# Casting the second layer's weights DRAM to DRAM during the first layer, and splitting the first layer's write-back over two blocks

## The chip, the cores and the metric

The kernel runs on all eight cores of one Trainium2 chip. Every core computes one sequence of the batch with its own copy of the weights' bf16 form, and no core waits for another. The metric is the device time of the slowest core in microseconds (us). A program of eight cores has a faster and a slower state: in some executions the cores of one die, or of both, get a lower TensorE clock, and the time is some per cent longer.

Engines: TensorE (PE: matmuls), VectorE (DVE), ScalarE (ACT), GpSimd (POOL) and SyncE (SP, which here only issues DMAs). A DMA issued by SyncE or ScalarE goes to one queue each; a DMA that changes the type, f32 to bf16, is issued by GpSimd and goes to a queue of its own (q0 in the profile; SyncE's is q1).

## The reference, cut to what matters

Two layers over 2048 tokens of width 2048, f32 inputs and weights:

```
shift, scale, gate = Linear(silu(c))              # adaLN
h   = x * (1 + scale) + shift
P   = h @ W_in                                    # 11.8k mixer columns, 8k merge-gate columns
y_A = Mamba-2 SSD; y_B = sliding-window attention
y_C = gated short convolution; y_D = RG-LRU
m   = sum_k sigmoid(G_k(h)) * (y_k @ W_branch[k])
x   = LayerNorm(alpha * x + gate * (m @ W_out))
```

Per layer there are 214 MB of f32 weights, 107 MB as bf16. MB and GB here are 10^6 and 10^9 bytes, as in the profile; only the sizes of single tiles and of single DMAs (KB, and the MB of `w`, `wg` and `wo` below) are counted in 1024s.

## The kernel before

Each layer works through four blocks of 512 tokens. The first half of a block makes `h` and the four branches and needs 92 weight tiles `w` (1 MB f32, 0.5 MB bf16). The second half merges and projects and needs 64 tiles `wg` (1.5 MB f32) and 16 tiles `wo` (1 MB f32). All operations are recorded in program order; then a list scheduler that runs when the kernel is built decides each engine's fixed order, by a key and by its own reckoning of durations. The second half of block s is keyed to run beside the first half of block s+1. I call this a pair: pair 0 is the second half of block 0 with the first half of block 1, and so on to pair 6. Blocks 0 to 3 are layer 0, blocks 4 to 7 are layer 1; so pair 3 holds the first half of layer 1's first block, pair 4 its second half.

The weights come as f32 and are multiplied as bf16. At a layer's first block each tile is cast on its way in, and written back as bf16 to scratch DRAM for the three blocks that follow:

```python
    def load_w(pool, l, first, src, scr, rscr, nel):      # first: t == 0
        w, rw = pool.get()
        wf = w.rearrange("p a b -> p (a b)")[:, 0:nel]
        if first:
            P.dma("pool", wf, src, writes=[rw], nbytes=128 * nel * 4)              # f32 -> bf16, on-chip
            P.dma("sp", scr, wf, reads=[rw], writes=[rscr], nbytes=128 * nel * 2)  # write-back
        else:
            P.dma("sp", wf, scr, reads=[rscr], writes=[rw], nbytes=128 * nel * 2)
        return w, rw
    ...
    NW1, NWG = 4, 3                                       # buffers for w, and for wg and wo
    ...
    for l in range(DEPTH):
        for t in range(NT):
            stage1(l, t)                                  # first half
            if prev is not None:
                stage2(*prev)                             # second half of the block before
            prev = (l, t)
```

adaLN for layer 0 (twelve blocks of w_ada, eight for scale and shift, four for the gate) runs at the start. That of layer 1 is spread over pairs 1 and 2.

The softmax here doesn't subtract the row's maximum and nothing guards it: scores larger than these inputs give would overflow.

Of the kernel before, what the change touches and what calls it, by code (L numbers as in the profile page):

```python
# [71 lines left out]
class Op:  # L72
    __slots__ = ("eng", "fn", "cost", "key", "idx", "preds", "order", "dma", "tbl", "succ", "osucc", "npred",
                 "ready", "sem", "val", "clk", "t0")


class Prog:


    LAT = {"pe": 0.20, "act": 0.22, "dve": 0.20, "pool": 0.25}  # L80
# [3 lines left out]
    DMA_RATE = 280e3  # L84
# [7 lines left out]
    def _add(self, e, fn, reads, writes, cost, acc, dma, tbl):  # L92
        o = Op()
        o.eng, o.fn, o.cost, o.key, o.idx, o.dma, o.tbl = e, fn, cost, self.key, len(self.ops), dma, tbl
        sync, order = set(), set()
        ops = self.ops
        isdma = dma is not None

        def need(i, war):
            p = ops[i]  # L100
            if war and p.dma is None and p.eng == e and not isdma and e == "pe":
                order.add(i)
            else:
                sync.add(i)
        for r in reads:
            for i in r.w:
                need(i, False)
            if r.excl:
                for i in r.r:
                    if ops[i].eng != e:  # L110
                        sync.add(i)
        for r in writes:
            if acc:
                for i in r.pw:
                    need(i, True)
                for i in r.pr:
                    need(i, True)
                for i in r.r:
                    need(i, True)
                if r.w and ops[r.w[-1]].eng == e and not isdma:  # L120
                    order.add(r.w[-1])
            else:
                for i in r.w:
                    need(i, e == "pe")
                for i in r.r:
                    need(i, True)
        k = o.idx
        for r in reads:
            r.r.append(k)
        for r in writes:  # L130
            if acc:
                r.w.append(k)
            else:
                r.pw, r.pr = r.w, r.r
                r.w, r.r = [k], []
        sync.discard(k)
        order.discard(k)
        o.preds, o.order = sync, order - sync
        ops.append(o)
        return o  # L140
# [4 lines left out]
    def dma(self, q, out, in_, reads=(), writes=(), nbytes=0, acc=False):  # L145
        return self._add(q, (out, in_), reads, writes, self.DMA_ISSUE[q], acc, nbytes, None)
# [93 lines left out]
    def emit(self, order):  # L240
        nc = self.nc
        sem = {k: nc.alloc_semaphore("s_" + k) for k in self.eng}
        cnt = {k: 0 for k in self.eng}
        seen = {k: {} for k in self.eng}
        dsem = {q: [[nc.alloc_semaphore("d_%s_%d" % (q, i)), 0, None] for i in range(n)]
                for q, n in self.DMA_SEMS.items()}
        dptr = {q: 0 for q in dsem}
        sems = {}
        last = {}
        ops = self.ops  # L250
        self.nwait = 0
        for o in order:
            e = o.eng
            eng = self.eng[e]
            sn = seen[e]
            slot = None
            ps = [ops[i] for i in o.preds]
            if o.dma is not None:
                slot = dsem[e][dptr[e] % len(dsem[e])]
                dptr[e] += 1  # L260
                if slot[2] is not None:
                    ps.append(slot[2])
            ps.sort(key=lambda p: -p.t0)
            for p in ps:
                if sn.get(p.sem, 0) < p.val:
                    eng.wait_ge(sems[p.sem], p.val)
                    self.nwait += 1
                    for kk, vv in p.clk.items():
                        if sn.get(kk, 0) < vv:
                            sn[kk] = vv  # L270
                    if sn.get(p.sem, 0) < p.val:
                        sn[p.sem] = p.val
            if o.dma is not None:
                slot[1] += 16
                s = slot[0]
                o.sem, o.val = s.name, slot[1]
                sems[s.name] = s
                eng.dma_start(out=o.fn[0], in_=o.fn[1]).then_inc(s, 16)  # L278
                slot[2] = o
            else:  # L280
                ins = o.fn(eng)
                cnt[e] += 1
                s = sem[e]
                sems[s.name] = s
                ins.then_inc(s, 1)
                o.sem, o.val = s.name, cnt[e]
            o.clk = dict(sn)
            last[o.sem] = o.val
        sp = self.eng["sp"]
        for nm, v in last.items():  # L290
            if seen["sp"].get(nm, 0) < v:
                sp.wait_ge(sems[nm], v)
# [15 lines left out]
def build_program():  # L308
# [5 lines left out]
    w_ada = dt_in("w_ada", [DEPTH, 12, NKC, 128, 512])  # L314
# [38 lines left out]
    PM = Pool("pm", [banks[b] for b in (0, 1, 2)])  # L353
    PJ = Pool("pj", [banks[b] for b in (3, 4)])
    PX = Pool("px", [banks[b] for b in (5, 6, 7)])
# [21 lines left out]
    NW1, NWG = 4, 3  # L377
# [61 lines left out]
    def c_dve(n):  # L439
        return 0.16 + n * 1.04e-3  # L440

    def c_act(n):
        return 0.18 + n * 0.85e-3
# [16 lines left out]
    def stt(out, in0, scalar, in1, op0, op1, reads, writes, n=512, acc=False):  # L460
        P.op("dve", lambda e: e.scalar_tensor_tensor(out=out, in0=in0, scalar=scalar, in1=in1, op0=op0, op1=op1),  # L461
             reads, writes, cost=c_dve(n) + 0.03, acc=acc)
# [25 lines left out]
    MMC = 0.2165  # L488

    def load_w(pool, l, first, src, scr, rscr, nel):  # L490
        w, rw = pool.get()
        wf = w.rearrange("p a b -> p (a b)")[:, 0:nel]
        if first:
            P.dma("pool", wf, src, writes=[rw], nbytes=128 * nel * 4)
            P.dma("sp", scr, wf, reads=[rw], writes=[rscr], nbytes=128 * nel * 2)
# [3 lines left out]

    def proj(l, t, hb, idx):  # L500
        w, rw = load_w(WS1, l, t == 0, w1_in[l, idx], w1s[l, idx], rW1S[l][idx], NKC * 128)
# [62 lines left out]
    def ada_piece(l, blk, kc, acc_t, slot, q):  # L564
        (a, ra), (w, rw) = acc_t, slot
        P.dma(q, w, w_ada[l, blk, kc], writes=[rw], nbytes=262144)
# [89 lines left out]
    def mix_a(l, t, setk):  # L656
# [35 lines left out]
        for g in range(4):  # L692
# [4 lines left out]
            for wi, (dst, rdst, col, ci) in enumerate(((bt, rbt, A_B, 8 + g), (ct, rct, A_C, 12 + g))):  # L697
                setk(6 * g + wi)
# [7 lines left out]
                if wi == 0:  # L706
# [6 lines left out]
                    PX.put((px, rpx))  # L713
            xs, zs, ya = [], [], []
            for i in range(2):
                j = 2 * g + i
                setk(6 * g + 2 + 2 * i)
# [8 lines left out]
                setk(6 * g + 3 + 2 * i)  # L726
# [4 lines left out]
                zs.append((z, rz))  # L731
            ya = [PX.get(), PX.get()]
            for u in range(4):
# [67 lines left out]
                HB.put((xe, rxe))  # L801
            BB.put((bc, rbc), (bt, rbt), (ct, rct))
# [22 lines left out]
    def mix_b(l, t, setk):  # L825
# [27 lines left out]
        for kc in range(2):  # L853
            setk(kc)
# [3 lines left out]
            for i in range(2):  # L858
                kh = 2 * kc + i
                P.dma("act", KD[64 - 64 * i:128 - 64 * i, kh, 128:640], KD[64 * i:64 * i + 64, kh, 128:640],  # L860
                      reads=[rKD[kh]], writes=[rKD[kh]], nbytes=65536)
        for v in range(2):
            setk(2 + v)
            idx = TIDX[B_V + 128 * v]
            w, rw = load_w(WS1, l, first, w1_in[l, idx], w1s[l, idx], rW1S[l][idx], NKC * 128)
# [7 lines left out]
            PJ.put((pj, rpj))  # L873
        for jq in range(8):
            kh = jq // 2
            setk(4 + 2 * jq)
# [4 lines left out]
            setk(5 + 2 * jq)  # L881
# [41 lines left out]
            F.put((f, rf))  # L923
        F.put((co, rco), (si, rsi))

    def mix_c(l, t, setk):
# [3 lines left out]
        for j in range(8):  # L930
            setk(4 * j)
# [4 lines left out]
            setk(4 * j + 1)  # L936
# [6 lines left out]
            setk(4 * j + 2)  # L943
# [6 lines left out]
            setk(4 * j + 3)  # L950
# [3 lines left out]
            F.put((a, ra))  # L954

    def mix_d(l, t, setk):
# [3 lines left out]
        for jp in range(4):  # L960
            st = []
            for j in (2 * jp, 2 * jp + 1):
                setk(2 * j)
# [27 lines left out]
            for j, (a, ra), (cv, rcv), (xs, rxs) in st:  # L991
                setk(2 * j + 1)
# [10 lines left out]
                F.put((a, ra), (cv, rcv), (xs, rxs))  # L1003


    def merge_dc(l, t, dc):
# [3 lines left out]
        for k in range(4):  # L1010
            idx = dc * 4 + k
            w, rw = load_w(WSG, l, t == 0, wg_in[l, idx], wgs[l, idx], rWGS[l][idx], 24 * 128)
# [25 lines left out]
    def out_dc(l, t, dc, sums):  # L1038
        s = l * NT + t
        b = s % 2  # L1040
        w, rw = load_w(WSG, l, t == 0, wo_in[l, dc], wos[l, dc], rWOS[l][dc], NKC * 128)
# [54 lines left out]
    def stage1(l, t):  # L1096
        s = l * NT + t
        P.key = s - 0.12
        make_h(l, t)
        base = [0]  # L1100

        def setk(i):
            P.key = s + (base[0] + i) / NTL
        setk(0)
        if t == 0:
            layer_consts(l)
        mix_a(l, t, setk)
        base[0] = 24
        mix_b(l, t, setk)
        base[0] = 44  # L1110
        mix_c(l, t, setk)
        base[0] = 76
        mix_d(l, t, setk)
# [22 lines left out]

    def stage2(l, t):
        s = l * NT + t
        tot = 64 * 24 + 256.0
        for dc in range(NKC):  # L1140
            P.key = s + 1 + 96 * dc / tot
            if l == 0 and t in (1, 2):
                ada_bg(6)
            merge_dc(l, t, dc)
        sums = (F2.get(), F2.get())
        for dc in range(NKC):
            P.key = s + 1 + (1536 + 16 * dc) / tot
            out_dc(l, t, dc, sums)
        P.key = s + 2
# [4 lines left out]
    ring = Pool("adaw", [take([512], F32, at=o_y[0] + i * 2048) for i in range(16)])  # L1154
    accs = Pool("adaa", [take([512], F32, at=o_y[1] + i * 2048) for i in range(12)])
    for _, r in ring.free_:
        pass
    alias0, alias1 = [], []
    for blk in range(12):
        P.key = -1.9 if blk < 8 else 0.4  # L1160
        acc_t = accs.get()
        for kc in range(NKC):
            slot = ring.get()
            alias0.append(slot[1])
            ada_piece(0, blk, kc, acc_t, slot, "sp" if kc % 2 == 0 else "act")
            ring.put(slot)
# [4 lines left out]
        if blk == 11:  # L1171
            ada_post(0, "gate")
# [21 lines left out]
    order = P.schedule()  # L1194
# [80 lines left out]
def make_in_maps(inp, cores):  # L1275
# [4 lines left out]
    wa = np.stack([wa[:, :, c:c + 512].reshape(DEPTH, NKC, 128, 512) for c in blocks], axis=1)  # L1280
# [35 lines left out]
```

## Time and profile before

The first three of the four runs gave 7065.18, 7064.13 and 7385.76 us; the last of these is a slow one. The lines below are from the profile's page: the span, TensorE's busy time with its share of the span and its instructions, and the DRAM traffic.

```profile
span 7077.5 us, 93078 instructions; the slowest of 8 cores (7022.1 to 7077.5 us)
PE 6284.8 (89%) x31128; PEld 2851.3 (40%) x31128; DVE 3735.2 (53%) x5916; ACT 2047.0 (29%) x3257; POOL 540.4 (8%) x1086
...
HBM read 1285.35 MB, written 249.82 MB: 217 GB/s over the span
```

TensorE is 89% busy. To see where the other 11% is, the next view cuts the span into stretches. I matched the recorded operations to the trace by their count on each engine's semaphore, and cut where the last matmul of each block's layer norm ends. Columns: from and to, length, busy time of each engine (with instructions), granted clock of TensorE, share of the DMA engines' time that is busy, GB/s that they moved (bytes written). The rows are start-up, block 0 alone, pairs 0 to 6, and the last second half.

```profile
core 7: us, PE busy (x) PEld busy (x) DVE busy (x) ACT busy (x) POOL busy (x), PEclk, DMA share, GB/s
0.00:265.00 265.00, 23.86 (x101) 22.10 (x102) 164.70 (x266) 13.49 (x22) 6.39 (x14) 1.00 0.92 249
265.00:894.00 629.00, 453.19 (x2151) 192.23 (x2148) 284.87 (x472) 181.12 (x296) 83.35 (x183) 0.87 0.84 176
894.00:1735.00 841.00, 762.54 (x3765) 342.42 (x3765) 414.70 (x647) 247.66 (x399) 79.87 (x168) 0.96 0.88 208
1735.00:2546.00 811.00, 782.34 (x3943) 358.01 (x3942) 494.61 (x786) 251.42 (x403) 59.39 (x93) 0.98 0.62 191
2546.00:3362.00 816.00, 778.54 (x3926) 355.97 (x3925) 489.86 (x777) 253.28 (x404) 56.85 (x93) 0.99 0.63 191
3362.00:4171.00 809.00, 769.55 (x3813) 349.46 (x3812) 427.28 (x685) 250.91 (x398) 81.34 (x184) 0.98 0.90 215
4171.00:5076.00 905.00, 815.75 (x4087) 368.19 (x4086) 451.14 (x734) 283.03 (x451) 87.25 (x180) 0.96 0.90 217
5076.00:5844.00 768.00, 740.61 (x3695) 337.23 (x3693) 409.45 (x631) 231.86 (x371) 35.16 (x83) 0.99 0.51 159
5844.00:6634.00 790.00, 768.88 (x3881) 350.69 (x3880) 427.76 (x674) 251.85 (x403) 50.77 (x88) 0.99 0.52 159
6634.00:7078.00 444.00, 389.48 (x1780) 175.03 (x1777) 170.84 (x247) 82.38 (x116) 0.00 (x0) 0.94 0.46 156
```

A pair without casts (5 and 6, mean 779 us) is 97% TensorE. Start-up, block 0 alone, pair 0 and pair 4 are longer.

The page's lines for DMAs (what, queue, count, KB each, median us from issue to landing) show what a weight buffer goes through at a layer's first block: the cast load, then the write-back.

```profile
arena<-wg POOLq DMA_DIRECT2D x128, 768.0 KB, 11.4
wg_scr<-arena SPq DMA_DIRECT2D x128, 768.0 KB, 10.3
arena<-w POOLq DMA_DIRECT2D x184, 512.0 KB, 9.3
w_scr<-arena SPq DMA_DIRECT2D x184, 512.0 KB, 8.5
```

### The profile page before, as it was taken

What the parts mean: (1) busy time and instruction counts of PE and PEld (TensorE: products, weight loads), DVE (VectorE), ACT (ScalarE), POOL (GpSimd) and SP (SyncE); (2) the same over time, 40 slices, a digit from 0 to 9 for tenths busy, and PEclk for the clock granted to TensorE, in tenths of its full rate; (3) what the DMA queues carried; (4) which work ended last, traced back from release to release, by engine and by line L of the source; (5) the groups of instructions that cost most, each with busy time, mean ns of one, the idle gap of its engine ahead of it and who ended that gap; (6) DMA issues with size and microseconds to landing.
All of it is one profiled execution on the core that took longest, in us unless ns stands there. A gap on an engine that the chain in (4) does not pass through costs nothing.

```text
span 7077.5 us, 93078 instructions; the slowest of 8 cores (7022.1 to 7077.5 us)
## 1 busy us (share of the span) xinstructions
PE 6284.8 (89%) x31128; PEld 2851.3 (40%) x31128; DVE 3735.2 (53%) x5916; ACT 2047.0 (29%) x3257; POOL 540.4 (8%) x1086
## 2 busy tenths in 40 slices
PE   0467788998999989999899988999799999999898
PEld 0232334343444434444344434444344444444343
DVE  5654345526775467635655365543575247643524
ACT  0231233214421243213432243213342134312312
POOL 0010111001100011000110001000010001000000
PEclk9988999999999999999999999999899999999999
DMA  9796989799665566556988999888854456544445
GB/s 260 187 184 153 205 190 212 198 215 242 196 188 190 177 208 194 174 191 183 212 214 205 221 229 207 214 214 206 226 165 142 152 170 188 155 142 161 147 152 162
DMA packets 409845, 1350.35 MB, mean 191 GB/s; under 512 B 49312, under 2 KB 60704, under 8 KB 409376
## 3 DMA queue, kind: packets, MB, share of 16 engines
q1 hardware_dynamic: 308736, 1048.25, 46.0%
q0 software_dynamic: 49824, 214.06, 19.9%
q10 hardware_dynamic: 50816, 82.09, 5.5%
q8 instruction: 257, 4.21, 0.2%
q14 instruction: 212, 1.74, 0.1%
HBM read 1285.35 MB, written 249.82 MB: 217 GB/s over the span
## 4 chain that ended last, share of the span: by engine, by line
PE 72%; DMA 12%; DVE 7%; issue 4%; ACT 3%; ACTq 1%; POOL 1%; SPq 0%; DVEq 0%; POOLq 0%
PE ps L481 72%; DMA arena<-cum_scr 4%; DVE arena L461 3%; DVE arena L457 2%; ACT arena L453 2%; DMA arena<-w 1%; DMA arena<-w_ada 1%; ACTq L278 1%; DVE arena L472 1%; DMA wg_scr<-arena 1%; DMA arena<-arena 1%; DMA arena<-pos 1%; DMA arena<-w_scr 1%; DMA arena<-x 1%; DMA arena<-x_scr 1%
## 5 line engine op out<-in xcount | busy, mean ns | idle before, releaser
L481 PE MATMUL ps<-arena 128*128 128x512 bf16 (+4 forms) x30744 | 6262.4, 366 | 740.5 <-DVE arena L461 307.0
L481 PEld LDWEIGHTS ps<-arena 128*128 128x128 bf16 (+2 forms) x30744 | 2816.3, 102 | 4138.8 <-issue 1279.3
L457 DVE TENSOR_TENSOR arena<-arena 128x512 f32<-128x512 f32 (+4 forms) x2466 | 1473.6, 624 | 635.6 <-ACT arena L453 418.3
L453 ACT ACTIVATE arena<-arena 128x512 f32<-128x512 f32 (+3 forms) x1495 | 946.0, 669 | 1495.0 <-DVE arena L461 384.2
L461 DVE SCALAR_TENSOR_TENSOR arena<-arena,ps 128x512 f32<-128x512 f32 (+1 forms) x832 | 565.2, 687 | 1354.0 <-PE ps L481 1035.1
L461 DVE SCALAR_TENSOR_TENSOR arena<-arena 128x512 f32<-128x512 f32 (+3 forms) x1283 | 934.2, 738 | 502.7 <-ACT arena L453 377.3
L453 ACT ACTIVATE arena<-ps 128x512 f32<-128x512 f32 (+3 forms) x960 | 538.5, 567 | 1660.4 <-PE ps L481 1413.8
L453 ACT ACTIVATE arena<-ps,arena 128x512 f32<-128x512 f32 x648 | 444.9, 687 | 1717.5 <-PE ps L481 1683.0
L457 DVE TENSOR_TENSOR arena<-ps,arena 128x256 bf16<-128x256 f32 (+5 forms) x616 | 262.2, 457 | 440.2 <-PE ps L481 434.9
L475 POOL COPY arena<-arena 128x3 f32<-128x3 f32 (+3 forms) x542 | 210.6, 392 | 3664.4 <-DVE arena L457 1676.2
L472 DVE RECIPROCAL arena<-arena 128x512 f32<-128x512 f32 x80 | 268.0, 3350 | 40.1 <-ACT arena L453 35.6
L461 DVE SCALAR_TENSOR_TENSOR arena<-ps,arena 128x512 f32<-128x512 f32 x136 | 100.3, 745 | 179.2 <-PE ps L481 178.1
L457 POOL TENSOR_TENSOR arena<-arena 128x512 f32<-128x512 f32 x128 | 138.6, 1084 | 564.0 <-DMA arena<-cum_scr 412.9
L278 POOL DMA_DIRECT2D arena<-w x184 | 98.1, 534 | 758.7 <-PE ps L481 608.3
L453 ACT ACT_TABLE_LOAD x58 | 74.4, 1283 | 152.9 <-DVE arena L457 66.0
L278 POOL DMA_DIRECT2D arena<-wg x128 | 68.7, 538 | 618.0 <-PE ps L481 445.0
L467 DVE TENSOR_SCALAR arena<-arena 128x512 bf16<-128x512 f32 (+4 forms) x191 | 62.1, 342 | 53.8 <-ACT arena L453 34.9
L486 PE MATMUL ps<-arena 128*128 128x128 f32 (+1 forms) x384 | 70.9, 270 | 21.8 <-DVE arena L461 11.1
L467 DVE TENSOR_SCALAR arena<-ps,arena 128x512 f32<-128x512 f32 x64 | 48.0, 750 | 65.8 <-PE ps L481 65.5
L995 DVE TENSOR_TENSOR_SCAN arena<-arena 128x512 f32<-128x512 f32 x64 | 78.2, 1255 | 0.1
L457 DVE TENSOR_TENSOR arena<-arena,ps 128x256 f32<-128x256 f32 x112 | 46.7, 417 | 34.6 <-PE ps L481 31.9
L486 PEld LDWEIGHTS ps<-arena 128*128 128x128 f32 (+1 forms) x384 | 40.2, 129 | 56.1 <-issue 35.8
(21 smaller groups left out, 138.9 us busy)
## 6 DMA issues: line engine op xcount, KB each, us to landing
arena<-wg_scr SPq DMA_DIRECT2D x384, 768.0 KB, 5.0
arena<-w_scr SPq DMA_DIRECT2D x552, 512.0 KB, 4.5
arena<-wg POOLq DMA_DIRECT2D x128, 768.0 KB, 11.4
wg_scr<-arena SPq DMA_DIRECT2D x128, 768.0 KB, 10.3
arena<-w POOLq DMA_DIRECT2D x184, 512.0 KB, 9.3
w_scr<-arena SPq DMA_DIRECT2D x184, 512.0 KB, 8.5
arena<-w_ada SPq DMA_DIRECT2D x288, 256.0 KB, 4.8
arena<-wo_scr SPq DMA_DIRECT2D x96, 512.0 KB, 3.8
```

The lines of the kernel that those rows point to most:

```text
L278: eng.dma_start(out=o.fn[0], in_=o.fn[1]).then_inc(s, 16)
L453: P.op("act", lambda e: e.activation(out=out, in_=in_, func=func, **kw), reads, writes, cost=c_act(n) + (0.09 if bias is not None and not ...
L457: P.op(eng, lambda e: e.tensor_tensor(out=out, in0=in0, in1=in1, op=op), reads, writes, cost=c_dve(n * (0.5 if fast else 1.0)), acc=acc)
L461: P.op("dve", lambda e: e.scalar_tensor_tensor(out=out, in0=in0, scalar=scalar, in1=in1, op0=op0, op1=op1), reads, writes, cost=c_dve(n) + ...
L467: return e.tensor_scalar(out=out, in0=in0, scalar1=s1, scalar2=None, op0=op0)
L472: P.op("dve", lambda e: e.reciprocal(out=out, in_=in_), reads, writes, cost=0.1 + n * 6.3e-3)
L475: P.op("pool", lambda e: e.tensor_copy(out=out, in_=in_), reads, writes, cost=cost, acc=acc)
L481: r = e.matmul(out, lhsT=lhsT, rhs=rhs, start=st, stop=sp_, skip_group_check=True)
L486: P.op("pe", lambda e: e.transpose(out=out, in_=in_, identity=ident), reads, writes, cost=cost, acc=acc)
L995: P.op("dve", lambda e, cv=cv, a=a, xs=xs, init=init: e.tensor_tensor_scan(out=cv[:, 0:T], data0=a[:, 0:T], data1=xs[:, 0:T], initial=init ...
```

## The change

Its intent: casting layer 1's weights while layer 0 computes, so that no block of layer 1 waits for cast loads and write-backs; halving the write-backs of block 0, where TensorE idles most; shortening the start; and giving TensorE branch C's matmuls while branch A's chain is waiting. Cut to its core:

```diff
-    DMA_RATE = 280e3
+    DMA_RATE = 310e3                       # of the scheduler; its engine costs change a little too
-    PM = Pool("pm", [banks[b] for b in (0, 1, 2)])        # PSUM banks 3/2/3 -> 2/2/4
+    PM = Pool("pm", [banks[b] for b in (0, 1)])
-    NW1, NWG = 4, 3
+    NW1, NWG = 3, 3
+    KEEP1 = KEEP2 = lambda idx: idx % 2
-    def load_w(pool, l, first, src, scr, rscr, nel):
+    def load_w(pool, l, t, keep, src, scr, rscr, nel):
...
-        if first:
+        if l == 0 and t <= keep:
             P.dma("pool", wf, src, ...)
-            P.dma("sp", scr, wf, ...)
+            if t == keep:                  # odd tiles: cast in blocks 0 and 1, written back in block 1
+                P.dma("sp", scr, wf, ...)
...
+    def cast_bg(n):                        # layer 1: all w, then all wg, then all wo
+        for _ in range(n):
+            nx = next(cast1, None)
+            if nx is None:
+                return
+            P.dma("pool", nx[1], nx[0], writes=[nx[2]], ..., after=[P.last_pe])
...
             merge_dc(l, t, dc)
+            if l == 0 and t in (2, 3):
+                cast_bg(4)                 # in out_dc's loop: cast_bg(2)
...
+            if l == 0 and t == 0:
+                ada_gate0(4)               # gate part of layer 0's adaLN, out of the start-up
...
-        mix_a(l, t, setk); mix_b(l, t, setk); mix_c(l, t, setk); mix_d(l, t, setk)
+        zip_run((mix_a(l, t), 40), (mix_c(l, t), 8))      # A and C recorded in turns
+        zip_run((mix_b(l, t), 12))
+        zip_run((mix_d(l, t), 4))
```

`KEEP` gives the last block at which a tile of layer 0 is still cast: even tiles as before, odd tiles are cast at blocks 0 and 1 and written back at block 1, so block 0 writes half as much. The start-up's w_ada loads also become 512 KB instead of 256 KB each. (The line with the four `mix_` calls is written shorter here than it stands.)

## The prediction

> **What bounds it now.** TensorE: busy 6285 of 7077 us (page, part 1). The kernel is a pipeline: start-up, first half of block 0 alone, seven pairs (second half of block s beside first half of block s+1), last second half alone. Cut where each pair's layer norm ends and read with the windows view (us; PE busy; clock; DMA share):
>
> - start-up 265; 24; DMA 0.95
> - block 0 alone, to 894: 629; 453; clock 0.81-0.99
> - pair 0: 840; 762; 0.96; 0.88
> - pair 1: 804; 778; 0.99; 0.62
> - pair 2: 816; 779; 0.99; 0.63
> - pair 3: 814; 772; 0.98; 0.90
> - pair 4: 906; 817; 0.96; 0.90
> - pairs 5, 6: 763, 790; 738, 769; 0.99; 0.51
> - tail 451; 394
>
> A clean pair is about 780 us and TensorE-bound. The excess lies in start-up, block 0 alone, pair 0 and pair 4: the f32 loads with write-back. A weight buffer is taken for cast load (11.4 us for wg, 9.3 for w) plus write-back (10.3, 8.5; DMA issues), so three wg buffers give a tile per 22/3 = 7.3 us against 5.2 of matmuls. In pair 4 the chain gives 6.6% to the wg write-back and GpSimd waits 115 us for it.
>
> **Step by step.**
> 1. Gate part of adaLN later: 4 of 12 blocks leave start-up, 15 us each (w_ada landings, DMA 280 GB/s). The input scaling reads a record that the gate writes, so it waited for it (until 261; scale and shift were done at 197). Wholly on the path: -63. Its 64 VectorE pieces (0.74 us each) go to pair 0, whose VectorE is half idle.
> 2. Branches A and C in turns: matters in block 0 alone. A's chain waits for cum_scr loads (13.8% of this stretch, 14-18 us each) while TensorE idles; C now fills it. Half the write-backs leave too, but w buffers fall from 4 to 3. TensorE needs some 375 us; VectorE chains and weights at 4.3-4.8 us a tile hold it near 510: -115. The Trainium skill (TensorE: Matmul & The Clock Gate, Part 1) says activity releases the throttle; the trace agrees (0.73-0.86 at 300-550 us, 1.00 when full), so less idling also quickens matmuls.
> 3. Split write-back: pair 0 loses half the wg write-backs but gains half-cast w tiles of block 1: -25. Pair 1 gets odd wg cast loads and write-backs, DMA share to 0.85: +5.
> 4. Layer-1 weights DRAM to DRAM: pair 4 becomes clean: -120; pair 3's first half reads bf16. The 172 casts (about 350 us of full DMA in each of pairs 2 and 3, from 0.324 us per 4 KB cast packet) ride on GpSimd's queue and hold no buffer. The Trainium skill (DMA: Bandwidth & Descriptors, SWDGE vs HWDGE vs iDMA) says an engine round-robins between queues, so weight loads slow but don't stop; no run shows it yet. Pair 2 +15, pair 3 +5.
> 5. PSUM 2/2/4 instead of 3/2/3, new scheduler costs: pairs 5, 6 and tail -10 in all.
>
> Sum -308: **6757 us** (4.4% faster), range 6630-6870. Faster over 2%: 0.94, same 0.05, slower 0.01.
>
> **Signs.** First dense matmuls near 200, not 265 us; block 0 alone ends near 710; pair 4 below 800 without write-backs in its chain; DMA share 0.9-1.0 in pairs 2 and 3 with PE still 94% busy; w_scr write-backs below 8 us.
>
> **What would break it.** Casts saturating DMA so that TensorE waits for w_scr and wg_scr loads in pairs 2-3 (+100); two merge banks stalling TensorE on ScalarE; three w buffers making block 0 load-bound (no gain there).

## More of the kernel before

Pair 4's 905 us needs care: it holds 4087 matmuls and pair 5 only 3695, while a pair's own work is about 3885. Some 200 matmuls of pair 5 stand in pair 4, about 44 us at the 0.217 us that a matmul takes in a full stretch (814 in 177 us).

## The result

The changed kernel took 7356.63 us as the median of four runs (7349.86, 7344.18 and 7363.40 fast, 7410.47 slow), beside 7065.18 and 7064.13 (fast), 7385.76 and 7248.04 us (slow) of the kernel before. The fast runs over the fast runs of the kernel before give 1.0407, with a 95% interval of 1.0374 to 1.0441: 4.1% slower. Such a ratio, here and below, is the mean time of one kernel's fast runs over that of the other's in the same rounds, so it is not quite the ratio of the medians. The same page lines after:

```profile
span 7348.8 us, 92520 instructions; the slowest of 8 cores (7296.7 to 7348.8 us)
PE 6361.1 (87%) x31128; PEld 2874.4 (39%) x31128; DVE 3737.4 (51%) x5916; ACT 2058.9 (28%) x3265; POOL 584.9 (8%) x1172
...
HBM read 1445.78 MB, written 249.82 MB: 231 GB/s over the span
```

DRAM reads rose by 160 MB: layer 1's bf16 weights are read back once more (107 MB), and the odd tiles of layer 0 are read as f32 a second time where they were read as bf16 (53 MB more). The stretches, in the same order as before:

```profile
0.00:189.00 189.00, 16.46 (x69) 14.94 (x70) 117.18 (x201) 13.42 (x22) 5.87 (x13) 1.00 0.89 258
189.00:733.00 544.00, 436.46 (x2151) 190.21 (x2149) 285.79 (x473) 183.05 (x301) 83.17 (x185) 0.93 0.80 157
733.00:1641.00 908.00, 784.59 (x3797) 350.20 (x3798) 449.04 (x712) 246.67 (x396) 111.91 (x215) 0.93 0.94 210
1641.00:2481.00 840.00, 785.42 (x3926) 358.35 (x3924) 498.27 (x785) 257.11 (x411) 78.25 (x132) 0.97 0.79 219
2481.00:3498.00 1017.00, 830.28 (x3927) 369.95 (x3924) 491.86 (x777) 251.47 (x400) 88.91 (x185) 0.89 0.85 195
3498.00:4499.00 1001.00, 805.55 (x3828) 356.37 (x3828) 428.40 (x686) 255.96 (x402) 71.06 (x169) 0.91 0.90 191
4499.00:5300.00 801.00, 769.66 (x3882) 352.82 (x3880) 432.85 (x682) 257.12 (x409) 54.91 (x93) 0.99 0.51 159
5300.00:6104.00 804.00, 772.19 (x3883) 353.06 (x3883) 433.88 (x683) 257.71 (x410) 46.55 (x93) 0.99 0.50 161
6104.00:6901.00 797.00, 768.86 (x3880) 352.09 (x3879) 428.76 (x674) 252.64 (x401) 44.29 (x87) 0.99 0.50 157
6901.00:7349.00 448.00, 391.62 (x1797) 176.42 (x1795) 171.40 (x248) 83.78 (x117) 0.00 (x0) 0.94 0.50 155
```

Start-up (189), block 0 alone (544) and pair 4 (801) fell about as hoped. Pairs 2 and 3, which carry the casts ahead, went from 816 and 809 us to 1017 and 1001 us; TensorE is busy only 830 and 806 us of them, and its granted clock fell to 0.89 and 0.91. Pairs 0 and 1 got longer as well. Who TensorE waited for in pairs 2 and 3 (who, for what: us in total, times, longest), first before, then after:

```profile
PE ps L481 <- ACT arena L453: 36.7, 17, 4.9
PE ps L481 <- DVE arena L457: 26.7, 13, 4.6
```

```profile
PE ps L487 <- DMA arena<-w_scr: 173.3, 29, 13.8
PE ps L487 <- ACT arena L459: 52.0, 17, 7.2
PE ps L487 <- DMA arena<-wo_scr: 45.9, 4, 17.4
PE ps L487 <- DMA arena<-wg_scr: 39.3, 6, 23.8
```

Before, TensorE waited there for no weight load at all. After, waits for w_scr, wo_scr and wg_scr loads sum to 258 us, and TensorE's busy time in the two pairs rose by 52 and 36 us at the lower clock. The chain of work in pair 2 (start, us, what) shows loads of 256 KB on it that take 21 and 26 us; loads of w_ada, for layer 1's adaLN, are 24.1% of the pair in that chain and loads of w_scr 15.0%:

```profile
2556.95 21.01 DMA arena<-w_ada
2595.09 26.02 DMA arena<-w_ada
```

The casts ahead themselves, issue to landing, by the page's lines for DMAs:

```profile
w_scr<-w POOLq DMA_DIRECT2D x92, 512.0 KB, 13.6
wg_scr<-wg POOLq DMA_DIRECT2D x64, 768.0 KB, 20.2
```

The packets in the trace show why I first suspected their size. A DRAM-to-DRAM tile of w goes as 16 packets of 32768 B, 3.47 us each on average in pair 2, where the cast loads of the kernel before were 4096 B packets of 0.32 us (median). At 2554.5 to 2556.0 us four casts are issued together; from 2560 to 2564 us the cast queue held 0.99 of the engines' time and SyncE's queue moved 1 GB/s. In that burst a load of 256 KB issued at 2556.95 us landed 21 us later, one issued at 2542.08 us had landed in 2.8 us.

Two theories and more were on the table:

- **G, granularity.** Each packet of a weight load waits behind one cast packet of 3.5 us.
- **P, bursts.** Four casts at once hold the engines for 20 us.
- **M (first called B and H), memory traffic.** The core has all the DRAM bandwidth that it gets, whatever the packets look like.
- **D.** The DMA engines or GpSimd's queue are full by themselves.
- **Something else in the change** (three w buffers, branch order, banks), with the casts innocent.

For M I counted the traffic of each pair. A bf16 load or write-back counts once, a cast load on-chip counts its f32 source (twice the bf16 bytes), a DRAM-to-DRAM cast counts source and destination (three times), an on-chip copy nothing; each DMA is spread from issue to landing. The sums are 1536 MB before and 1699 MB after; the page's DRAM totals are 1535 and 1696 MB (a recount from the sizes in the traces gives exactly these). By this count pair 2 carried 154 MB before and 294 MB after, pair 3 220 and 303 MB.

### The profile page after: what moved, and what is told of

Its sections match the earlier page's. It is cut to its first block, busy times and chain, and to the rows that moved or that the text cites. A ratio compares the mean times of both kernels' runs of the same rounds, so it can differ in the third digit from the quotient of the medians.

```text
span 7348.8 us, 92520 instructions; the slowest of 8 cores (7296.7 to 7348.8 us)
## 1 busy us (share of the span) xinstructions
PE 6361.1 (87%) x31128; PEld 2874.4 (39%) x31128; DVE 3737.4 (51%) x5916; ACT 2058.9 (28%) x3265; POOL 584.9 (8%) x1172
## 4 chain that ended last, share of the span: by engine, by line
PE 60%; DMA 26%; DVE 6%; issue 4%; ACT 2%; ACTq 1%; SPq 1%; POOL 0%; DVEq 0%; another core or an unknown queue 0%; POOLq 0%
PE ps L487 60%; DMA arena<-w_scr 8%; DMA arena<-w_ada 5%; DVE arena L463 3%; DMA arena<-cum_scr 2%; DVE arena L467 2%; ACT arena L459 2%; DMA arena<-w 2%; DMA arena<-wg_scr 2%; DMA arena<-arena 1%; ACTq L282 1%; DMA w_scr<-arena 1%; DMA arena<-x_scr 1%; DMA arena<-wg 1%; DMA arena<-x 1%
## 5 line engine op out<-in xcount | busy, mean ns | idle before, releaser
L487 PE MATMUL ps<-arena 128*128 128x512 bf16 (+5 forms) x30744 | 6343.8, 369 | 945.8 <-DVE arena L467 251.0
L463 DVE TENSOR_TENSOR arena<-arena 128x512 f32<-128x512 f32 (+6 forms) x2466 | 1473.6, 625 | 566.8 <-ACT arena L459 297.9
L467 DVE SCALAR_TENSOR_TENSOR arena<-arena 128x512 f32<-128x512 f32 (+2 forms) x1283 | 943.6, 742 | 849.0 <-ACT arena L459 547.9
L459 ACT ACTIVATE arena<-ps 128x512 f32<-128x512 f32 (+4 forms) x960 | 535.3, 567 | 1708.6 <-PE ps L487 1644.8
L481 POOL COPY arena<-arena 128x3 f32<-128x3 f32 (+4 forms) x542 | 219.0, 406 | 3310.8 <-DVE arena L463 1117.5
L282 POOL DMA_DIRECT2D arena<-w x138 | 73.8, 536 | 537.7 <-PE ps L487 476.9
L282 POOL DMA_DIRECT2D arena<-wg x96 | 51.8, 541 | 475.6 <-PE ps L487 446.5
L282 POOL DMA_DIRECT2D w_scr<-w x92 | 44.7, 491 | 336.8 <-PE ps L487 334.0
```

The costliest lines, as they stand in the source:

```text
L282: o.ins = eng.dma_start(out=o.fn[0], in_=o.fn[1])
L459: P.op("act", lambda e: e.activation(out=out, in_=in_, func=func, **kw), reads, writes, cost=c_act(n) + (0.09 if bias is not None and not ...
L463: P.op(eng, lambda e: e.tensor_tensor(out=out, in0=in0, in1=in1, op=op), reads, writes, cost=c_dve(n * (0.5 if fast else 1.0)), acc=acc)
L467: P.op("dve", lambda e: e.scalar_tensor_tensor(out=out, in0=in0, scalar=scalar, in1=in1, op0=op0, op1=op1), reads, writes, cost=c_dve(n) + ...
L481: P.op("pool", lambda e: e.tensor_copy(out=out, in_=in_), reads, writes, cost=cost, acc=acc)
L487: r = e.matmul(out, lhsT=lhsT, rhs=rhs, start=st, stop=sp_, skip_group_check=True)
```

## The experiments

All times of pairs are read as above, on one core whose trace has every semaphore record; cores of one run differ by up to some 20 us in most pairs, and by more in a few. Where the core that was read is not typical, the median over all eight cores is given beside it; for that, block 0 alone runs from the first dense matmuls to the last f32 matmul of the block's first half, and pairs are cut at the last f32 matmul of the layer norm. Chips differ between the groups of runs, so a ratio is to the kernel before in the same rounds.

### First group: packets, or the casts as such

**e1_rows.** Every cast walks the rows of its tile in a strided order, so that rows can't be merged:

```diff
-            P.dma("pool", nx[1], nx[0], writes=[nx[2]], ...)
+            rows = lambda a: a.rearrange("(r h b) c -> h r (b c)", h=16, b=1)
+            P.dma("pool", rows(nx[1]), rows(nx[0]), writes=[nx[2]], ...)
```

> The changed kernel with one edit: each DRAM-to-DRAM cast walks its rows in a strided order, so that rows cannot be merged and a packet should be one row (4096 or 6144 B written) instead of 32768 or 24576 B. Bytes, casts, pacing and queue stay. Theory G (granularity: each packet of a weight load waits at its DMA engine behind one 3.4 us cast packet): pairs 2 and 3 fall from 1017 and 1001 us to about 840 each, w_scr waits of TensorE there go from 45 and 128 us to under 15, total 7000 to 7060 us. Rival theory B (bandwidth: 204 MB more read in two pairs whose DMA engines were 0.6 busy): the bytes are the same, so both pairs stay near 1000 us and the total near 7350.

The packets became 4096 B (322 ns at the fast end, 453 ns on average), as meant. The time did not follow: 7302.99 to 7316.44 us in four fast runs, ratio 1.0317 (1.0252 to 1.0383). Pairs 2 and 3:

```profile
2441.00:3397.00 956.00, 808.01 (x3852) 364.52 (x3925) 493.32 (x777) 252.24 (x401) 92.83 (x185) 0.93 0.92 212
3397.00:4374.00 977.00, 804.43 (x3756) 356.32 (x3829) 430.62 (x685) 255.86 (x402) 71.69 (x169) 0.92 0.91 192
```

Pair 2 gained 61 us and pair 3 24 us; some 300 us of their 393 us of extra time stay. Over all eight cores pair 2 has 1012 us in the changed kernel and 968 here, pair 3 997 and 985. Granularity is at most a small part of it. Theory G falls as the main cause.

**e2_two_rows.** The same with `b=2`.

> As e1_rows, but two rows stay together: packets of 8192 and 12288 B written. Theory G: a weight load has 8 packets per engine, each behind one cast packet of about 0.7 to 1.0 us, so 6 to 8 us more per load; that mostly fits in the buffers' lead: pairs 2 and 3 between 840 and 900 us, a little above e1_rows and far below 1000. Theory B: near 1000 us each, as in e1_rows.

Packets were 8192 B; the fast runs took 7323.47 and 7316.69 us, pairs 2 and 3 991 and 983 us. Packet sizes from 4 to 32 KB span about 60 us in pair 2.

**e3_no_ahead.** The changed kernel without the casts ahead; layer 1 casts and writes back at its first block.

```diff
-        if l == 0 and t <= keep:
+        if t <= (keep if l == 0 else 0):
             P.dma("pool", wf, src, ...)
-            if t == keep:
+            if t == keep or l == 1:
                 P.dma("sp", scr, wf, ...)
...
-                cast_bg(4)
+                pass                       # and the same for cast_bg(2)
```

> The changed kernel without the casts ahead: layer 1's weights are cast and written back at its first block as in the kernel before; all other parts of the change stay. Both theories: pairs 2 and 3 back to about 820 us, pair 4 up to about 900, total 7030 to 7090 us. If pairs 2 and 3 stay near 1000, the casts are not the cause at all but the other parts (3 w buffers, branch order, banks).

Three of its four runs fell into the slow state, among them the profiled one. The one fast run took 7036.09 us, in the range expected. The profiled run can be read in part, for its lower clock comes in stretches: on cores 0 and 1 the granted clock was 0.97 to 0.98 in both pair 2 and pair 3 (and 0.82 in pair 4). Pairs 2 and 3 on core 1:

```profile
2477.00:3311.00 834.00, 783.69 (x3926) 360.75 (x3925) 490.31 (x777) 251.59 (x400) 45.37 (x92) 0.98 0.59 184
3311.00:4153.00 842.00, 776.07 (x3827) 350.58 (x3827) 427.57 (x685) 252.98 (x399) 84.00 (x185) 0.98 0.85 210
```

Without the casts, and with everything else of the change in place, they are back at 834 and 842 us (core 0: 839 and 830). e7_w_once below shows the same in a fast run. So of the 393 us some 340 go with the casts ahead; the other parts of the change account for some 50 (834 and 842 against 816 and 809).

**e4_ahead_alone.** The kernel before plus `cast_bg` and its calls, nothing else of the change.

> The kernel before with the casts ahead alone (its 4 w buffers, its branch order, banks and scheduler costs stay). If the casts by themselves cost it: pairs 2 and 3 near 1000 us each, pair 4 about 800, total 7280 to 7380 us. If it takes the cast together with 3 w buffers or the new order, it comes out near or under the 7065 us of before.

The fast runs took 7325.58 and 7361.48 us, ratio 1.0364 (1.0227 to 1.0501), with 1006 us in pair 2, 978 in pair 3 and 792 in pair 4. Pair 2:

```profile
2532.00:3538.00 1006.00, 813.31 (x3928) 362.92 (x3927) 496.08 (x777) 258.20 (x410) 103.55 (x185) 0.91 0.89 206
```

So the casts ahead alone, on the old kernel with four w buffers and the old order, cost the 4%; nothing else in the change is needed for it.

### Second group: pace, amount, and the split of w

**e5_paced.** The casts of e1_rows, but one after each merge step (four per column, about 10 us apart) instead of four together.

```diff
+            if l == 0 and t in (2, 3):     # in merge_dc, after each k
+                cast_bg(1)
...
             merge_dc(l, t, dc)
-            if l == 0 and t in (2, 3):
-                cast_bg(4)
...                                        # in out_dc's loop: one, and two more after odd columns
```

> e1_rows showed that packet size is not it: packets of 4096 B, pairs still near 1000 us. Left: theory H (traffic: a pair takes about the longer of 790 us and its memory traffic over some 295 GB/s; a DRAM-to-DRAM cast counts three times its bf16 bytes, so pair 2 carries 294 MB and pair 3 303 MB) and rival theory P (bursts: four casts at once hold the DMA engines some 20 us, and the weight loads behind them arrive too late). Here the same casts in 4096 B packets go out one at a time, one after each merge step, same bytes. Theory P: w_scr and w_ada waits vanish, pairs 2 and 3 fall to 850 us or less, total under 7080. Theory H: pairs 2 and 3 stay at 970 to 1010 us, total 7250 to 7330.

The fast runs took 7286.53 to 7294.50 us, ratio 1.0311 (1.0267 to 1.0355). Pairs 2 and 3:

```profile
2478.00:3435.00 957.00, 812.23 (x3852) 366.77 (x3924) 495.91 (x777) 251.25 (x401) 96.41 (x185) 0.93 0.91 207
3435.00:4424.00 989.00, 805.19 (x3755) 358.80 (x3828) 431.72 (x685) 256.60 (x402) 74.44 (x169) 0.90 0.94 193
```

Nothing gained over e1_rows: 957 and 989 us against 956 and 977. Theory P falls. By my count the core carried 306 to 307 GB/s through both pairs.

**e6_half.** Every second tile of layer 1 is cast ahead, the others as in the kernel before.

```diff
+        if l == 1:
+            keep = 0 if keep == 0 else -1
...
-    cast1 = iter([... for i in range(NTL)] + ...
+    cast1 = iter([... for i in range(1, NTL, 2)] + ...     # wg and wo likewise; cast_bg(2) and cast_bg(1)
```

> The changed kernel with every second layer-1 tile cast ahead (paced two at a time), the others cast and written back at layer 1's first block as before. Theory H: memory traffic per pair about 222 MB (pair 2), 263 MB (pair 3), 190 MB (pair 4), so 800 to 830, 890 to 920 and 800 to 830 us, total 7080 to 7150. Theory P (bursts of two, half as long): both pairs near 850, total about 7050. If the cost went with the number of casts alone, pairs 2 and 3 would each come out near 900.

The one fast run took 7107.67 us. In the profiled run die 0 was slow (0.87), die 1 undisturbed (0.96 to 0.97); pairs 2 and 3 on core 6 of die 1:

```profile
2490.00:3335.00 845.00, 780.21 (x3853) 358.52 (x3927) 490.74 (x778) 251.26 (x400) 66.86 (x139) 0.97 0.79 209
3335.00:4212.00 877.00, 781.20 (x3757) 352.80 (x3828) 428.69 (x684) 253.72 (x400) 80.27 (x177) 0.96 0.88 209
```

Pair 2 carried 225 MB, pair 3 260 MB. The 877 us of pair 3 lie just under the expected 890, the 845 of pair 2 above the expected 830 (core 7 of the same die had 862 and 891; core 6 has the shortest pair 2 of the four, their median is 859 us, and 881 in pair 3). Half the casts cost far less than half of what all of them cost in pair 2: 859 us against 839 without any (e7_w_once, below, median of eight cores) and 1012 with all. One fixed cost per cast does not fit that, a limit on traffic does.

**e7_w_once.** As e3_no_ahead, and only wg and wo are split over two blocks; w is cast once and written back at block 0.

```diff
-    KEEP1 = KEEP2 = lambda idx: idx % 2
+    KEEP1, KEEP2 = (lambda idx: 0), (lambda idx: idx % 2)
```

> The changed kernel without casts ahead and with the split write-back for wg and wo alone (each w tile of layer 0 is cast once, at block 0). Theory H: pair 0 carries 219 instead of 266 MB and falls from 907 to about 840 us; block 0 alone gains 23 MB of write-backs and 10 to 20 us; pair 1 stays near 840; total about 6980 to 7010, under the 7036 us of the fast run of e3_no_ahead. If pair 0 stays near 900, its loss comes from the three w buffers, the branch order or the gate pieces instead.

6991.09 and 7015.38 us in the fast runs, ratio 0.9905 (0.9828 to 0.9981). Block 0 alone, pair 0 and pair 4:

```profile
190.00:781.00 591.00, 451.58 (x2149) 194.19 (x2148) 287.28 (x473) 184.32 (x300) 81.31 (x183) 0.89 0.86 185
781.00:1595.00 814.00, 758.58 (x3793) 345.41 (x3791) 447.30 (x711) 243.36 (x392) 88.97 (x171) 0.97 0.85 203
4116.00:4934.00 818.00, 773.87 (x3883) 355.46 (x3882) 432.93 (x683) 258.01 (x411) 92.89 (x170) 0.98 0.95 229
```

Against the changed kernel, block 0 alone gave back 47 us (544 to 591, more than expected) and pair 0 gained 94 (908 to 814); over all eight cores it is 40 and 92 us. So the split of w took from pair 0 twice what it gave to block 0: those tiles cross DRAM again as f32 (266 MB in pair 0 against 217).

**e8_split_both.** As e7_w_once, with layer 1's wg and wo split as well.

```diff
-        if t <= (keep if l == 0 else 0):
+        if t <= keep:
             P.dma("pool", wf, src, ...)
-            if t == keep or l == 1:
+            if t == keep:
```

> As e7_w_once, with the split write-back of wg and wo for layer 1 too: no casts ahead at all, odd wg and wo tiles of layer 1 are cast in pairs 4 and 5 and written back in pair 5. Traffic by theory H: pair 4 225 instead of 250 MB, pair 5 about 167 MB, all under 230 MB. Pair 4 falls from about 890 to 810 to 840 us, pair 5 stays near 800; total 6900 to 6960: faster than both kernels. If the write-backs of pair 4 do not matter, it equals e7_w_once.

A miss: 7033.24 and 7036.39 us, ratio 0.9949 (0.9907 to 0.9992), slower than e7_w_once. Pair 4 went from 818 to 827 us and pair 5 from 810 to 846. Pair 4 of e7_w_once was short already, so the halved write-backs had nothing to give there, and pair 5 took the second casts.

### Third group: what runs out, and the smaller parts

**e9_sbuf_source.** A probe with a wrong result (relative error 0.053): the 172 casts ahead read a zeroed on-chip tile, not the f32 weights.

```diff
-            P.dma("pool", nx[1], nx[0], writes=[nx[2]], ...)
+            for h in range(nx[3] // 8):
+                P.dma("pool", nx[1][:, 1024 * h:1024 * h + 1024], ZSRC, reads=[rZS], writes=[nx[2]],
+                      ..., acc=h > 0, after=[P.last_pe])
```

> A probe with a wrong result on purpose: the changed kernel, but its 172 ahead casts read a zeroed on-chip tile of 1024 f32 per partition (a 4 KB row, 2048 B packets, two or three transfers per weight tile) instead of the f32 weights in DRAM. The DMA engines still move every written byte through the same cast on the same queue; DRAM traffic per weight tile falls from 1.5 to 0.5 MB (w). It tells what runs out in pairs 2 and 3. Theory M (memory traffic: some 295 to 300 GB/s per core with all eight running): traffic falls to about 200 MB per pair, so pairs 2 and 3 fall to 830 to 870 us. Theory D (time of the DMA engines or GpSimd's queue by itself): they stay near 980 us.

7124.27 and 7069.07 us, ratio 1.0059 (0.9985 to 1.0133). Pairs 2 and 3:

```profile
2516.00:3346.00 830.00, 781.17 (x3926) 358.90 (x3925) 490.45 (x777) 253.00 (x404) 158.05 (x285) 0.98 0.88 240
3346.00:4183.00 837.00, 774.26 (x3827) 351.69 (x3826) 429.78 (x685) 253.28 (x403) 147.74 (x305) 0.96 0.86 229
```

They fall to 830 and 837 us. GpSimd issued more transfers than in the changed kernel (158 and 148 us of busy time against 89 and 71), every written byte still went through the same queue and the same cast, and the DMA engines were as busy (0.88 and 0.86 against 0.85 and 0.90). What left is the reading of the f32 weights from DRAM: 198 and 188 MB in the two pairs by my count instead of 294 and 303. Theory D falls and theory M stands: what the two pairs paid for is this reading from DRAM, and a DMA share near 0.9 is no limit by itself. Three things to know of the probe: its packets are of 2048 B (e1_rows showed that small packets alone do not bring it); from the first half of pair 3 on layer 1 multiplies by zeros, so pair 2 is the cleaner reading; and block 0 alone, which the edit does not touch, got 50 us longer (medians 540 and 590), so the scheduler's order moved elsewhere too. In pairs 2 and 3 the numbers of matmuls are those of the changed kernel, and all eight cores have 827 to 844 and 822 to 837 us.

**e10_four_w.** e7_w_once with `NW1 = 4`.

> e7_w_once with four w buffers as in the kernel before (two f work buffers fewer). If three w buffers hold back block 0 alone, whose w tiles are cast and written back there, it falls from 591 to 550 to 565 us, about where the split put it (544), and pairs 1 and 2 (848, 833) stay; total near 6960. If not, 585 or more.

No gain: 6995.26 to 7017.60 us, ratio 0.9933 (0.9901 to 0.9964), block 0 alone 584 us. Three w buffers are not what holds it.

**e11_in_sequence.** e7_w_once with the branches recorded one after the other.

```diff
-        zip_run((mix_a(l, t), 40), (mix_c(l, t), 8))
-        zip_run((mix_b(l, t), 12))
-        zip_run((mix_d(l, t), 4))
+        for g in (mix_a(l, t), mix_b(l, t), mix_c(l, t), mix_d(l, t)):
+            zip_run((g, 1))
```

> e7_w_once with branches A, B, C, D recorded one after the other as in the kernel before. My theory of the turns: they gain in block 0 alone (TensorE idle in A's chain) and cost in the pairs, where TensorE already had other work: block 0 alone rises from 591 to 620 to 640 us, pairs 1, 2 and 5 fall from 848, 833 and 810 to about 815, 815 and 790; the total moves under 1%. If the turns are neutral in the pairs, those stay, and the total is 30 to 50 us worse.

My theory of the turns fell: 7001.37 to 7006.32 us, ratio 0.9928 (0.9895 to 0.9961), as e7_w_once. Block 0 alone was 592 us (591 with the turns), pair 0 839 (814; over eight cores 820 and 813), pairs 1, 2 and 5 846, 838 and 800 (848, 833, 810). The turns did nothing for the stretch that I expected them to shorten.

**e12_old_rate.** e7_w_once with `DMA_RATE = 280e3`, a number that only the scheduler uses.

> e7_w_once with one constant of the scheduler set back: the DMA rate that it reckons with, 280 instead of 310. In e7_w_once pair 4 takes 818 us although it casts and writes back as in the kernel before, where it took 905. Theory O (order): at the lower rate the scheduler believes pair 4's weights late, lets the first half of the next block run ahead and leaves the merges for later; the recorded order of TensorE shows this. Then pair 4 goes up to 860 us or more, of which pair 5 gives back up to 30. If pair 4 stays near 820, its gain has another cause (banks, buffers, turns).

6958.67 to 6967.80 us in three fast runs, ratio 0.9872 (0.9846 to 0.9897). Pair 4 did go up, to 901 us on die 1 of the profiled run (die 0 was slow). But the whole got faster, which I had not expected.

### Fourth group: a control, a few casts ahead, no split

**e12_again.** The file of e12_old_rate once more.

> Control, the same file as e12_old_rate: 6950 to 6970 us, pairs 1 to 4 near 809, 818, 786 and 901 us.

6960.43, 6948.08 and 6948.93 us, ratio 0.9823 (0.9780 to 0.9867): 1.8% faster than the kernel before, the best of all (whether by over 2% is within the interval). Pairs 0 and 4:

```profile
787.00:1581.00 794.00, 752.49 (x3793) 345.37 (x3794) 449.50 (x711) 242.61 (x391) 81.99 (x171) 0.98 0.86 208
3998.00:4904.00 906.00, 827.45 (x4166) 377.42 (x4165) 466.76 (x745) 292.79 (x464) 88.21 (x184) 0.96 0.92 224
```

Pair 4 holds 4166 matmuls, in e7_w_once 3883: at the lower rate the scheduler lets 283 matmuls of the neighbouring pairs run in pair 4, some 61 us. Pairs 3 to 5 sum to 2465 us here (786, 906, 773) and to 2468 us in e7_w_once (840, 818, 810). So theory O holds for the order, and the order was worth nothing in these three pairs. The gain is in pairs 0 to 2 (794, 819, 812 against 814, 848, 833; over eight cores 54 us for the three together). It is not all kept: block 0 alone is some 30 us longer at the lower rate (over eight cores 611 against 580; 607 on the six undisturbed cores of e12_old_rate, which ran on the chip of e7_w_once). Why the other order is better in these pairs and worse in block 0 alone I have not found.

**e13_few_ahead.** The control with 21 wg tiles cast ahead, in pair 2 alone.

```diff
+    AHEAD = range(1, 64, 3)
...
+        if l == 1:
+            keep = -1 if (pool is WSG and nel == 24 * 128 and scr_ahead(rscr)) else 0
...
+            if l == 0 and t == 2:
+                cast_bg(1 + dc % 2)
```

> The control with 21 of the 64 wg tiles of layer 1 cast ahead, one or two per merge column of pair 2 alone. Traffic of pair 2 rises from 152 to about 203 MB (250 GB/s), that of pair 4 falls from 241 to about 208 MB. Theory M (the casts cost only where the traffic nears 300 GB/s): pair 2 rises by at most 25 us, pair 4 falls from 901 to 830 to 870 us, total 20 to 50 us below the control. Rival: a cast ahead costs in proportion, about 2.2 us each as in pairs 2 and 3 of the changed kernel: pair 2 +46 us, the total equal or worse.

6961.23 and 6977.05 us, ratio 0.9852 (0.9788 to 0.9917): not faster than the control. Pair 2 rose from 812 to 844 us at 201 MB (239 GB/s), a little more than the 25 us expected. Pair 4 fell from 906 to 834, and pair 5 rose from 773 to 801, as pair 4 no longer held its matmuls. Pairs 2 to 5 sum to 3259 us against 3277, which the whole time, that of the slowest core, doesn't show. Here a cast ahead cost about 1.5 us (32 us over 21 casts; over eight cores 819 to 844 us, 1.2 us a cast) although the traffic was far from 300 GB/s; theory M as I stated it does not explain that, and e9_sbuf_source paid nothing at the same traffic (830 us against 833). Part of it can be seen in the trace: in pair 2's chain of work loads of w_ada are 5.7% of the pair and loads of w_scr 4.8%, single ones of 15 to 22 us, where the control has 2.6% of w_ada. So single loads still come late beside casts although the mean traffic is low.

**e14_no_split.** The control with `KEEP1 = KEEP2 = lambda idx: 0`.

> The control with the split write-back undone for wg and wo too: all of layer 0 is cast once and written back at block 0. Traffic: pair 0 about 241 instead of 217 MB, pair 1 about 160 instead of 210 MB. If the split pays as predicted: pair 0 +25 us or more, pair 1 unchanged to -10, total 15 to 40 above the control. If it is neutral: within 10 us of the control.

7069.67 and 7079.44 us, ratio 1.0002 (0.9948 to 1.0055): all the gain of the control is gone. Pair 0:

```profile
819.00:1727.00 908.00, 806.02 (x4018) 366.06 (x4016) 464.42 (x756) 265.14 (x426) 85.63 (x179) 0.95 0.89 220
```

Pair 0 takes 908 us (4018 matmuls, 225 of them from pair 1, which falls to 788). Over block 0 alone and pairs 0 and 1 the split of wg and wo is worth 110 us (623 + 908 + 788 against 596 + 794 + 819), about 100 by the medians of eight cores, with pair 0 going from 907 to 800. That is several times what the prediction gave it.

A choice of pairs, by traffic (MB by my count, us, GB/s; not all pairs counted stand here):

| kernel, pair | MB | us | GB/s |
|---|---|---|---|
| before, pair 2 | 154 | 816 | 189 |
| e9_sbuf_source, pair 3 | 188 | 837 | 225 |
| e9_sbuf_source, pair 2 | 198 | 830 | 239 |
| e13_few_ahead, pair 2 | 201 | 844 | 239 |
| e6_half, pair 2 | 225 | 845 | 267 |
| e7_w_once, pair 4 | 240 | 818 | 294 |
| e6_half, pair 3 | 260 | 877 | 296 |
| changed kernel, pair 0 | 266 | 908 | 293 |
| changed kernel, pair 2 | 294 | 1017 | 289 |
| e5_paced, pair 2 | 294 | 957 | 307 |
| changed kernel, pair 3 | 303 | 1001 | 303 |
| e5_paced, pair 3 | 303 | 989 | 306 |

The length rises little up to some 240 MB and much from 260 MB on; no pair in the table, or of e1_rows, got over 312 GB/s (e1_rows, pair 2, 298 MB in 956 us). Lengths at the low end also differ by the scheduler's order (see e12_old_rate), so the table shows a highest mean over a pair, not a threshold. The Trainium skill (HBM Reference, Specifications (TRN2)) gives an effective 358 GB/s per core when both cores of a domain stream. Averaged over a whole pair, 303 to 312 GB/s was all. But this mean is no limit at every moment: by the packets' times, counted as above, 28% of the 10 us stretches in pair 2 of the changed kernel carried more than 358 GB/s, the highest 601; over 100 us it was at most 324. So what is shown is that the pairs pay for the casts' reads from DRAM and that no pair sustained more than about 310 GB/s; what makes the mean stop there is not shown.

## Why the prediction was wrong

Term by term, predicted and measured, in us (the sums differ from the median's change because these are the two profiled runs):

| term | predicted | measured |
|---|---|---|
| start-up | -63 | -76 |
| block 0 alone | -115 | -85 |
| pair 0 | -25 | +67 |
| pair 1 | +5 | +29 |
| pair 2 | +15 | +201 |
| pair 3 | +5 | +192 |
| pair 4 | -120 | -104 |
| pairs 5, 6, tail | -10 | +47 |
| sum | -308 | +271 |

- **Step 4 failed, and it decides the sign.** It read "weight loads slow but don't stop" and put +15 and +5 on pairs 2 and 3; they cost +201 and +192. I had costed the casts in time of the DMA engines ("about 350 us of full DMA"), taken from packets of the kernel before, and found room. That size was right: the casts' packets took 324 and 415 us of all 16 engines in the two pairs. (The 0.324 us named there is a median and gives only some 260 us; 350 comes out with the means, 0.43 us for 4 KB and 0.65 for 6 KB.) The room that mattered was DRAM traffic: each cast ahead adds its f32 source and its bf16 result on top of loads that go on, and the bf16 has to be read again later. Pairs that carried 154 and 220 MB carried 294 and 303 MB. 303 MB in the 780 us of a clean pair would have asked for 388 GB/s, more than the Trainium skill (HBM Reference, Specifications (TRN2)), which I had read, gives a core (358); I did not make that division. e4_ahead_alone shows that the casts do it alone, e3_no_ahead that it goes with them, e9_sbuf_source that it is their reading from DRAM.
- **The claim drawn from the skill** (DMA: Bandwidth & Descriptors, SWDGE vs HWDGE vs iDMA: an engine round-robins between its queues) let me hope for an even share. With 32768 B packets SyncE's queue fell to 1 GB/s within a burst. With 4096 B packets it got more while casts ran (a mean of 74 GB/s in pair 2 over the 4 us stretches in which the cast queue held over half of the engines' time, against 38), and the pairs were still 956 and 977 us. A larger share of the turns did not bring the time back.
- **The named danger was right, its odds and size were not.** "Casts saturating DMA so that TensorE waits for w_scr and wg_scr loads in pairs 2-3 (+100)" is what happened, at +393 in all.
- **The sign chosen for step 4** was "DMA share 0.9-1.0 in pairs 2 and 3 with PE still 94% busy". The share came out 0.85 and 0.90; TensorE was busy 82% and 80%. e9_sbuf_source has the same DMA share with TensorE busy 94% and 93%, so the share could not have told right from wrong.
- **Step 1 held in start-up**: the first half of block 0 began at 189 us instead of 265. The prediction did not count that the gate's 16.8 MB then cross DRAM in pair 0. In e14_no_split, which keeps the late gate but no split and no casts ahead, start-up, block 0 alone and pairs 0 and 1 sum to 2515 us against 2546 before, so at most about 30 of the 76 us seem to be left. That kernel differs in more than the gate, so this is not shown for the gate alone.
- **Step 2 had about the right size for the wrong reason.** Block 0 alone fell by 85 (91 over eight cores), but e11_in_sequence shows that the turns gave at most some 12 us of it (591 against 580, medians; none on the cores read), and e10_four_w that the fourth buffer doesn't matter. By the medians the split of w gave 40 (e7_w_once), the scheduler's new DMA rate some 30 (e12_old_rate and e12_again against e7_w_once), which the prediction did not count here, and the split of wg and wo 11 (e14_no_split against e12_again; 27 on the two cores read). The write-backs of w, forecast to land in under 8 us, took 9.0.
- **Step 3 had both parts wrong.** The split of wg and wo is worth 100 to 110 us, much more than thought, and the split of w costs pair 0 94 us for 47 us in block 0 alone. I had noted that pair 0 "gains half-cast w tiles" and still put it at -25 in all; in traffic these tiles are 49 MB more (266 against 217).
- **Step 4's gain in pair 4 was measured, but is not all a gain.** 801 us against 905, yet the 905 included some 200 matmuls of pair 5. Pairs 4 and 5 together fell by 68 us (1673 to 1605), not by 120. This is also most of why "pairs 5, 6 and tail" missed: pair 5 seems 36 us longer because it now holds its own work.
- **The clock** behaved as predicted, to the kernel's harm. The Trainium skill (TensorE: Matmul & The Clock Gate, Part 1) says that activity releases the throttle; here waiting for weights took pairs 2 and 3 from 0.99 and 0.98 to 0.89 and 0.91, so the idle time also slowed the matmuls between.

What stays open: why the scheduler's lower rate gives a better order in pairs 0 to 2, why a cast ahead cost 1.2 to 1.5 us far below 300 GB/s in e13_few_ahead and next to nothing in e9_sbuf_source, and what sets the mean of about 310 GB/s that no pair passed: reads, writes or their mix, and whether the limit is the core's own or shared with other cores, since every run kept all eight cores busy.

## What to carry to other kernels

Before moving work into the background of a stretch, count the bytes that cross DRAM in it, reads and writes, not the busy share of the DMA engines, and divide by the stretch's length: a DRAM-to-DRAM cast from f32 counts three times its bf16 size, and its result is read once more. Compare it with the most that a stretch of the same kernel has sustained, here about 310 GB/s. Staying below that is not enough: e13_few_ahead paid 25 to 32 us at 239 GB/s. Test background transfers with a probe that keeps the transfers but takes one side off the memory; it tells traffic from queues and engines in one run. Compare stretches of a fixed schedule only with the count of matmuls beside them, as work moves over the cut.

## What the Trainium skill lacked or had wrong

- DMA: Bandwidth & Descriptors: the page makes a packet the turn between queues and prefers at most 4096 B for it, without saying how long a turn can get. A DRAM-to-DRAM cast of 128 contiguous rows went as packets of 32768 B (24576 B for wg) of 3.47 us on average, and while four of them ran, another queue fell to 1 GB/s and its 256 KB load took 21 us instead of 2.8. Nor does the page say that contiguous rows in DRAM are merged into such packets; a strided order of rows kept them at 4096 B (e1_rows).
- HBM Reference: the page has no figure for mixed traffic. Over pairs of 800 to 1000 us with reads, casts and write-backs mixed on eight cores, no pair read got over 312 GB/s; single 10 us stretches went up to 601 GB/s by count.
- No page that I read says what a cast costs in traffic: a DRAM-to-DRAM cast to bf16 counts three times the bytes that the profile's queue line shows. With that count the sums agree with the page's DRAM totals (1536 against 1535 MB, 1699 against 1696 MB).
